# Encoder block: one half of W_out split early and kept in DRAM, and the other half's sixteen pieces spread over the attention heads

## The chip, the cores and the metric

The kernel runs on one core of a Trainium2 chip. The metric is the time of one execution in device microseconds (us); a lower one is better. The engines are called as in the profile: PE (TensorE), DVE (VectorE), ACT (ScalarE), POOL (GpSimd) and SP (SyncE, which here only issues transfers).

## What is computed

The reference is one block on x of 1024 rows and 1024 columns, in float32, cut here to what matters:

```python
x = LN1(alpha*x + 0.5 * (silu(x @ w_gate1) * (x @ w_up1)) @ w_down1)      # hidden width 4096
z = x @ w_in                                                              # q, k, v, two LRU inputs, forget gates
for h in range(8):                                                        # 8 heads of width 64
    s = q_h @ k_h.T / 8 + cum_h[t] - cum_h[s]                             # cum = cumsum(log_sigmoid(forget gate))
    fox[:, 64*h:64*h+64] = softmax(where(s <= t, s, -1e30)) @ v_h
lru = gelu(z_lg) * rg_lru(conv(z_lx))                                     # a linear recurrence, width 512
x = LN2(alpha*x + concat(fox, lru) @ w_out)                               # w_out: 1024 x 1024
x = LN3(alpha*x + 0.5 * (silu(x @ w_gate2) * (x @ w_up2)) @ w_down2)
```

`w_out` has two halves: its first 512 rows are multiplied with the attention's output (the attention half), its last 512 with that of the recurrence (the LRU half).

## The kernel before

**Products in three parts.** Each float32 operand is split into a high part (an ACT copy that casts to the fast type) and a low part (a DVE subtraction of the high part from the whole). `mm3` makes a product of three matmuls, high with high, high with low and low with high (L151 to L153). Splitting weights is thus work for ACT and DVE, and each split needs the weights' raw copy in SBUF first.

**Stages.** The program runs through FFN 1 (gate and up, then down), the mixer (input projections, the recurrence, the attention, the product with `w_out` and the second layer norm) and FFN 2. A framework lays each engine's instructions out in a fixed order by what each needs and when it was written; each engine then takes its own row in order and waits where an operand or a buffer isn't ready.

**Gate and up** (`gate_up`): sixteen pairs of 128-column blocks of the hidden width. Each pair is seven block products for gate and seven for up, each of 12 matmuls of 128x512. Their weights come as 1 MB loads into two raw buffers, are combined and split by ACT (L273) and DVE (L274) into a ring of 16 buffers (eight of high and low), and POOL stores the pair's results to DRAM (`h_d`, L543 and L544). While PE is busy with one pair, the weights of the next are made.

**Attention** (`attention`): 64 units, each a head h and a block i of 128 queries. Heads 0 to 5 run one after another, i from 7 down to 0; heads 6 and 7 are interleaved. A unit has these steps, and the names in brackets are used below.

- Scores (S h.i): matmuls L964 and L965 into PSUM; DVE adds the cumulated gates and takes the row's extreme (L970), ACT exponentiates (L971), POOL scales (L973). POOL also masks the diagonal block of the gates' row, which was loaded once per head (L968).
- Transposes (T h.i), three units later: up to 8 on PE (L984), copied and split by ACT (L988) and DVE (L989).
- Values (V h.i, for even i, two query blocks at once): matmuls L1000, then ACT (L1003) and DVE (L1004); for odd heads also a split of the finished pair of heads (L1007, L1008), which POOL stores to DRAM (`mix_d`, L1011).

Each head's q, k, v and gates are loaded by SP (L947 to L952) into one of two sets of buffers.

**The two halves of the output product.** The LRU half is 16 pieces (`fill`): 8 row blocks times 2 column halves, each of 4 times 3 = 12 matmuls of 128x512 (`down_tile`, L151 to L153) and one DVE addition. They depend on nothing in the attention and are written between the units: at units 0 to 4, then at every eighth unit plus 2, 3 and 4 (10 to 12, 18 to 20, 26 to 28) and at 34 and 35. The attention half is made at the end, in `out_tile`, as heads 6 and 7 get finished: again 16 pieces of 12 matmuls, M16 and on here; a row block's second piece is followed by its layer norm.

**W_out's attention half.** `out_w(w_out, 0)` loads its raw rows in two transfers of 1 MB (L929) and splits them in four steps at units 45, 47, 49 and 51, each a cast of 128x1024 by ACT (L143) and a subtraction by DVE (L144). The results lie in a pool of eight buffers, all of which hold the LRU half until that half's last pieces are through. At units 46, 48 and 52, SP loads the finished heads' parts back (`mix`, L1058), into another pool of eight that held the recurrence's output, the LRU half's other operand. SP takes its transfers in its own row as well: one that waits for a buffer holds up all behind it.

The functions before, with the line numbers of the profile:

Of the kernel before, what the change touches and what calls it, by code (L numbers as in the profile page):

```python
# [9 lines left out]
F32 = mybir.dt.float32  # L10
F32R = mybir.dt.float32r
# [6 lines left out]
P = 128  # L18
D = 1024
# [29 lines left out]
def f32(ap):  # L49
    return ap.bitcast(F32)  # L50


class Block:
# [202 lines left out]

        return raws, load

    def gate_up(self, wg, wu, h_d, rows, bank, tp, wsp, raws, later=None, aside=None):

# [256 lines left out]
        def halves(r):  # L519
            return r[:, 0:H], r[:, H:]  # L520

        pending = None
        for pair in range(FF // P // 2):
            if pair == 0:
                g0, h0, first, fifth, g1, h1, u = (self.row() for _ in range(7))
                homes = list(zip(halves(first), halves(first), halves(fifth)))
                gate, up = Matrix((g0, g1), *homes[0]), Matrix((h0, h1), *homes[1])
            else:
                g0, g1, uu, h0, h1, u = (self.row() for _ in range(6))
                gate, up = (Matrix(r, r[1][:, 0:H], x, r[0][:, H:]) for r, x in zip(((g0, g1), (h0, h1)), halves(uu)))  # L530
            def finish(pair=pair, g=(g0, g1), h=(h0, h1), u=u):
                for x, y in zip(h, g):
                    v.tensor_tensor(x, x, y, ALU.mult)
                (a11, a21), (a12, a22) = (halves(x) for x in h)
                s5 = g[0][:, 0:H]
                v.tensor_tensor(u[:, 0:H], a11, a22, ALU.add)
                v.tensor_tensor(u[:, H:], a21, a22, ALU.add)  # L537
                v.tensor_tensor(s5, a11, a12, ALU.add)
                v.tensor_tensor(a21, a21, a11, ALU.subtract)
                v.tensor_tensor(a12, a12, a22, ALU.subtract)  # L540
                d = h_d[pair // 4][:, pair % 4].rearrange("r p t -> p r t")
                for n, t in enumerate((*h, u)):
                    nc.gpsimd.dma_start(d[:, 2 * n:2 * n + 2], t.rearrange("p (r t) -> p r t", r=2))  # L543
                return nc.gpsimd.dma_start(d[:, 6], s5)  # L544

            def end(pair=pair, finish=finish):
                store = finish()
                if aside is not None and pair == 2:
                    with self.tc.issue_after(store.ins):
                        aside()  # L550

            if pair == 0:
                with self.tc.manual_schedule(engines=ENGINES) if later else nullcontext():
                    first_pair(gate, up)
                silu((g0, g1))
                end()
                continue
            for m, view in zip((gate, up), self.gu_views(wg, wu)):
                weights(pair, view, m.w)
            for m in (gate, up):  # L560
                m.one()
                if pending:
                    pending()
                for step in ("two", "six", "five", "seven", "three"):
                    getattr(m, step)()

                def pending(m=m, gate=gate, g=(g0, g1), end=end, last=pair == FF // P // 2 - 1):
                    m.four()
                    if m is gate:
                        silu(g)  # L570
                    elif not last:
                        end()
# [347 lines left out]

    def out_w(self, w_out, row0):

        wv = w_out.rearrange("(f p) d -> p f d", p=P)
        for c in range(2):
            r = self.raw([P, 2, D])
            f0 = row0 // P + 2 * c
            self.nc.sync.dma_start(r, wv[:, f0:f0 + 2, :])  # L929
            for j in range(2):  # L930
                yield tuple(t[:, 0, :] for t in self.split_ws(r[:, j:j + 1, :], 1))

    def attention(self, w_out, mixp, ln, normed):

        nc, v = self.nc, self.nc.vector
        mm = nc.tensor.matmul
        lru_tiles = list(zip(self.mix_lru, self.out_w(w_out, FOX)))
        with self.pool("att_p", 3) as pp, self.pool("att_t", 1) as tp, self.pool("att_pt", 6) as ptp, self.pool("att_qk", 2, side="right") as qkp:

            def load(h):  # L940
# [50 lines left out]
            def values(h, qt):  # L991
# [13 lines left out]
                if b:  # L1005
# [3 lines left out]
                    if qt == 0 and h < HEADS - 1:  # L1009
                        for l in range(2):  # L1010
# [4 lines left out]
            units = [(h, i) for h in range(HEADS - 2) for i in reversed(range(NT))]  # L1015
            units += [(6 + h, i) for h, i in ((0, 7), (0, 6), (0, 5), (0, 4), (1, 7), (1, 6), (0, 3), (0, 2),
                                              (1, 5), (1, 4), (0, 1), (0, 0), (1, 3), (1, 2), (1, 1), (1, 0))]
            tiles, mix, w_fox, w_steps = [], [], [], self.out_w(w_out, 0)
            MIXES = 46, 48, 52
            fill = [(i, d) for i in range(NT) for d in range(2)]  # L1020
            AHEAD = 3
# [9 lines left out]
            for n in range(len(units) + AHEAD + 1):  # L1031
                if n < len(units):
                    h, i = units[n]
                    if i == 5 and h < 6 or (h, i) == (6, 6):
                        heads[h + 1] = load(h + 1)
                    if i == NT - 1:
                        if h % 2 == 0:
                            outs[h // 2] = tp.tile([P, T], F32, tag="o", name=self.nm("o"))
                        else:
                            mixes[h // 2] = tuple(mixp.tile([P, T], F32R, tag="h", name=self.nm("mix")) for _ in range(2))  # L1040
                    ps[n] = probs(h, i)
                if 0 <= n - AHEAD < len(units):
                    to_pT(*units[n - AHEAD], ps.pop(n - AHEAD))
                if 0 <= n - AHEAD - 1 < len(units):
                    h, i = units[n - AHEAD - 1]
                    if i % 2 == 0:
                        values(h, i // 2)
                        if h == HEADS - 1:
                            tiles += [(i + 1, 0), (i + 1, 1), (i, 0), (i, 1)]
                if fill and (n < 2 or n % 8 in (2, 3, 4)):  # L1050
                    i, d = fill.pop(0)
                    self.down_tile(i, lru_tiles, 1.0, (d,))
                if 45 <= n < 53 and n % 2:
                    w_fox.append(next(w_steps))
                if n in MIXES:
                    mix.append(tuple(self.hp.tile([P, T], F32R, tag="h", name=self.nm("mix")) for _ in range(2)))
                    for l in range(2):
                        nc.sync.dma_start(f32(mix[-1][l]), mix_d[len(mix) - 1][l])  # L1058
                    if len(mix) == 3:
                        self.load_gb(*ln, [self.hp.tile([P, T], F32, tag="h", name=self.nm("gb")) for _ in range(2)])  # L1060
                if tiles:
                    out_tile()
# [4 lines left out]
def kernel(  # L1067
# [9 lines left out]
    xf = x[0]  # L1077
    h_d = [[blk.dram.tile([7, 4, P, H], F32, name=f"h{n}{q}_d") for q in range(4)] for n in range(2)]
    x2_d = blk.dram.tile([T, D], F32, name="x2_d")
    REST = ("s1", "s2", "s4", "s3")  # L1080

    with blk.pool("xl", side="right") as xl, blk.pool("x1") as x1, blk.pool("gu_t", 4) as tp, blk.pool("x22") as x22, \
            blk.pool("gu_ws", 16) as wsp, blk.banks() as bank, ExitStack() as inner:
        blk.open_blocks(x1, ("1",))
        blk.open_blocks(x22, ("22",))
        blk.open_blocks(xl, ("s3", "s1", "s2"))
        rows = [blk.row() for _ in range(4)]
        x2 = inner.enter_context(ExitStack())
        xp = x2.enter_context(blk.pool("x2", 4, side="right"))
        rows += [xp.tile([P, D], F32, tag="x2", name=blk.nm("x2")) for _ in range(4)]  # L1090

        def open_s4():
            x2.close()
            blk.open_blocks(inner.enter_context(blk.pool("s4", side="right")), ("s4",))

        raws, load = blk.first_raws(ffn1_w_gate[0], ffn1_w_up[0])
        warm = bank()
        for _ in range(12):
            nc.tensor.transpose(warm[:, 0:P], blk.ident, blk.ident)
        for i in range(NT):  # L1100
            if i == 4:
                load(0)
                load(1)
            nc.sync.dma_start(rows[i], xf[i * P:(i + 1) * P, :])

        finish = blk.gate_up(ffn1_w_gate[0], ffn1_w_up[0], h_d[0], rows, bank, tp, wsp, raws, open_s4, lambda: blk.mixer_consts(
            conv_w[0], conv_b[0], rg_wa[0], rg_ba[0], rg_wx[0], rg_bx[0], lru_lambda[0], b_forget[0], w_in[0]))
    with blk.psum():
        left = ExitStack()
        blk.wsp = left.enter_context(blk.pool("mx_ws", 8))  # L1110
        with blk.pool("dn_v", side="right") as vp, blk.pool("dn_w", side="right") as wp:
            first = []

            def hooks(norm):
# [3 lines left out]
                def columns(*offs):  # L1118
# [12 lines left out]
            blk.mixer_in(w_in[0], *first, [lambda i=i: blk.to_xT(i, False) for i in range(4, NT)])  # L1131
        mp = left.enter_context(blk.pool("mxp", 2))
        blk.fetched = None
        tiles, out_tile = blk.attention(w_out[0], mp, (ln2_g[0], ln2_b[0]),
                      lambda i: nc.gpsimd.dma_start(x2_d[(i + 4) % NT * P:((i + 4) % NT + 1) * P, :], blk.acc[i]))
        rows = blk.acc[4:] + blk.acc[:4]
        right = ExitStack()
# [59 lines left out]
```

## Time and profile before

| | before |
|---|---|
| median of 3 runs | 2354.17 us (2351.85 to 2358.68) |
| the profiled execution | 2350.71 us |
| its span in the trace | 2349.0 us, mean granted clock 0.998 |
| PE busy | 2305.3 us (98%) |
| DVE busy | 1631.3 us (69%) |
| ACT busy | 1011.6 us (43%) |
| POOL busy | 223.1 us (9%) |

The profiled execution has 1.7 us outside its span. The clock column of the views, PEclk, is the share of full speed that TensorE was granted. "Idle before" with an engine, a tile and a line says how long an engine stood still ahead of an instruction, and which other instruction it had waited for. A view by windows cuts the span at given times and gives each engine's busy time in each stretch, then the granted clock, the DMA engines' busy share and their rate.

### The profile page before, as it was taken

Reading aid. Unit: us, or ns where it says so; the run is one execution under the profiler, and the core shown is the slowest. Engines: PE = TensorE matmul, PEld = TensorE weight load, DVE = VectorE, ACT = ScalarE, POOL = GpSimd, SP = SyncE. Lnnn points to the kernel's source line nnn. Section 1 sums busy time; section 2 is a strip of 40 time slices with the busy share of each in tenths; the row PEclk is TensorE's granted clock in tenths of the full one; section 3 lists DMA queues with packets and bytes.
Section 4 is the critical chain, followed back from the end, with each engine's and each line's share of the span. In section 5 each row is a group of like instructions: output and inputs, shape, how many; then the busy total and the mean of one; then the engine's idle time right before and its main releaser. Section 6 shows DMA issues by size and latency. Waiting matters only on the chain.

```text
span 2349.0 us, 28311 instructions
## 1 busy us (share of the span) xinstructions
PE 2305.3 (98%) x10721; PEld 1914.4 (81%) x10721; DVE 1631.3 (69%) x2512; ACT 1011.6 (43%) x1587; POOL 223.1 (9%) x364
## 2 busy tenths in 40 slices
PE   9999999999999999999999899999999999999997
PEld 7788888888888888888878677888888888788886
DVE  7766566666567888766657899665656566478787
ACT  5443333434344345544446745434333333344341
POOL 0020000000000000111134510000000000000000
PEclk9999999999999999999999999999999999999999
DMA  3433232323466434232365812332323232564532
GB/s 121 139 90 126 91 117 85 117 86 117 145 240 215 161 115 120 60 109 91 118 174 149 237 54 86 103 117 86 118 92 126 86 117 86 198 247 156 196 108 90
DMA packets 175832, 298.93 MB, mean 127 GB/s; under 512 B 8192, under 2 KB 100672, under 8 KB 175696
## 3 DMA queue, kind: packets, MB, share of 16 engines
q1 hardware_dynamic: 152624, 218.15, 29.2%
q0 software_dynamic: 23072, 78.97, 9.1%
q8 instruction: 84, 1.38, 0.2%
q14 instruction: 52, 0.43, 0.1%
HBM read 214.22 MB, written 82.87 MB: 126 GB/s over the span
## 4 chain that ended last, share of the span: by engine, by line
PE 91%; DVE 5%; issue 1%; DMA 1%; ACT 1%; POOL 1%; SPq 0%; POOLq 0%; ACTq 0%; DVEq 0%
PE x L153 10%; PE x L152 9%; PE x L151 9%; PE b L152 7%; PE b L153 7%; PE b L151 7%; PE s L153 6%; PE s L152 6%; PE s L151 6%; PE a L151 6%; PE a L153 6%; PE a L152 5%; PE a L1000 1%; PE a L984 1%; PE a L873 1%
## 5 line engine op out<-in xcount | busy, mean ns | idle before, releaser
L273 ACT CAST ws<-t 128x512 fp32r<-128x512 f32 x240 | 148.9, 623 | 389.5 <-PE b L152 269.1
L273 ACT CAST ws<-raw 128x512 fp32r<-128x512 f32 x180 | 111.8, 623 | 260.0 <-PE x L152 256.6
L274 DVE TENSOR_TENSOR ws<-raw,ws 128x512 fp32r<-128x512 f32 x180 | 123.8, 688 | 142.7 <-ACT ws L273 139.3
L274 DVE TENSOR_TENSOR ws<-t,ws 128x512 fp32r<-128x512 f32 x240 | 164.4, 686 | 70.5 <-ACT ws L273 68.5
L151 PE MATMUL b<-As,ws 128*128 128x512 f32 x512 | 199.8, 390 | 3.0 <-ACT As L309 2.8
L151 PE MATMUL a<-ws,ws 128*128 128x512 f32 x512 | 199.2, 390 | 2.1 <-ACT ws L607 1.6
L151 PE MATMUL x<-As,ws 128*128 128x512 f32 x512 | 199.5, 390 | 1.0 <-ACT ws L273 1.0
L153 PE MATMUL x<-As,ws 128*128 128x512 f32 x512 | 199.4, 390 | 0.7 <-DVE ws L274 0.6
L152 PE MATMUL a<-ws,ws 128*128 128x512 f32 x512 | 199.5, 390 | 0.5 <-DVE ws L608 0.5
L152 PE MATMUL b<-As,ws 128*128 128x512 f32 x512 | 199.4, 390 | 0.2 <-DVE As L315 0.2
L153 PE MATMUL b<-As,ws 128*128 128x512 f32 x512 | 199.4, 389 | 0.0
L152 PE MATMUL x<-As,ws 128*128 128x512 f32 x512 | 199.2, 389 | 0.0
L153 PE MATMUL a<-ws,ws 128*128 128x512 f32 x512 | 199.2, 389 | 0.0
L151 PE MATMUL x<-A,ws 128*128 128x512 f32 x496 | 193.2, 390 | 1.1 <-ACT ws L273 1.1
L153 PE MATMUL x<-A,ws 128*128 128x512 f32 x496 | 193.3, 390 | 0.9 <-DVE ws L315 0.7
L152 PE MATMUL x<-A,ws 128*128 128x512 f32 x496 | 193.0, 389 | 0.0
L607 ACT CAST ws<-raw 128x1024 fp32r<-128x1024 f32 x112 | 117.4, 1050 | 161.5 <-PE a L152 87.8
L543 POOL DMA_DIRECT2D h_d<-row x96 | 68.8, 719 | 1155.6 <-DVE row L537 1116.5
L608 DVE TENSOR_TENSOR ws<-raw,ws 128x1024 fp32r<-128x1024 f32 x112 | 136.4, 1220 | 54.0 <-ACT ws L607 53.4
L151 PE MATMUL s<-ws,ws 128*128 128x512 f32 x384 | 149.5, 389 | 0.0
L153 PE MATMUL s<-ws,ws 128*128 128x512 f32 x384 | 149.4, 389 | 0.0
L152 PE MATMUL s<-ws,ws 128*128 128x512 f32 x384 | 149.4, 389 | 0.0
(248 smaller groups left out, 5227.8 us busy)
## 6 DMA issues: line engine op xcount, KB each, us to landing
raw<-h_d SPq DMA_DIRECT2D x56, 1024.0 KB, 5.5
h_d<-row POOLq DMA_DIRECT2D x96, 512.0 KB, 3.7
wd<-in_ffn_w_down_dram SPq DMA_DIRECT2D x32, 1024.0 KB, 7.8
raw<-in_ffn_w_gate_dram SPq DMA_DIRECT2D x30, 1024.0 KB, 5.5
raw<-in_ffn_w_up_dram SPq DMA_DIRECT2D x30, 1024.0 KB, 5.4
h_d<-row POOLq DMA_DIRECT2D x32, 256.0 KB, 2.6
raw<-in_w_in_dram SPq DMA_DIRECT2D x16, 512.0 KB, 5.2
row<-in_x_dram SPq DMA_DIRECT2D x12, 512.0 KB, 8.9
```

The lines of the kernel that those rows point to most:

```text
L151: mm(out, ah, bh, start=first, stop=False, skip_group_check=goes_on)
L152: mm(out, ah, bl, start=False, stop=False, skip_group_check=goes_on)
L153: mm(out, al, bh, start=False, stop=last, skip_group_check=goes_on)
L273: nc.scalar.copy(hi, src)
L274: v.tensor_tensor(lo, src, f32(hi), ALU.subtract)
L543: nc.gpsimd.dma_start(d[:, 2 * n:2 * n + 2], t.rearrange("p (r t) -> p r t", r=2))
L607: nc.scalar.copy(hi, src)
L608: self.mark = v.tensor_tensor(lo, src, f32(hi), ALU.subtract)
L873: nc.tensor.matmul(pa[:, 0:width], xl, wh[:, 0:width], start=False, stop=k == KT - 1)
L984: nc.tensor.transpose(pa[:, (j % 4) * P:(j % 4 + 1) * P], p[:, j * P:(j + 1) * P], self.ident)
L1000: mm(pv[:, ps], vt[:, j, :], pts[h, qt][j // 4][l][:, j % 4, ps], start=j == 0 and l == 0, stop=j == last and l == 1)
```

## The change

The first FFN's `gate_up` gets the attention half of `w_out` as a `spare`. At pairs 5 and 9, behind the pair's weights, `split_spare` loads 1 MB of it into a raw buffer, splits it in four blocks of 128x512 with the same ACT and DVE instructions as the weights, into buffers of the same ring, and POOL stores the eight results (256 KB each) to a new DRAM tensor, `fox_d`. Together that is 2 loads, 8 casts, 8 subtractions and 16 stores. At units 45, 47, 49 and 51, `out_w_parts` now loads finished parts from `fox_d`, 512 KB for the high and 512 KB for the low, in place of the raw loads, casts and subtractions. And the LRU half's 16 pieces are written at units 0 to 5 and then at every fourth, 8, 12, and so on to 44.

```diff
+        def split_spare(c):
+            w, w_d = spare
+            r = self.raw([P, KT, 2 * P]).rearrange("p k c -> p (k c)")
+            nc.sync.dma_start(r.rearrange("p (f d) -> p f d", f=2), w.rearrange("(f p) d -> p f d", p=P)[:, 2 * c:2 * c + 2])
+            for j in range(2):
+                for d in range(2):
+                    cols = slice(j * D + d * H, j * D + (d + 1) * H)
+                    for l, t in enumerate(parts(r[:, cols].rearrange("p (k c) -> p k c", k=4))):
+                        nc.gpsimd.dma_start(w_d[2 * c + j, l][:, d * H:(d + 1) * H], f32(t).rearrange("p k c -> p (k c)"))
...
                 weights(pair, view, m.w)
+            if spare and pair in (5, 9):
+                split_spare(pair // 8)
...
+    def out_w_parts(self, w_d):
+        w = [self.wsp.tile([P, 4 * VW], F32R, tag="ws", name=self.nm("w"))[:, 0:D] for _ in range(2)]
+        for l in range(2):
+            self.nc.sync.dma_start(f32(w[l]), w_d[l])
+        return w
...
-            tiles, mix, w_fox, w_steps = [], [], [], self.out_w(w_out, 0)
+            tiles, mix, w_fox = [], [], []
...
-                if fill and (n < 2 or n % 8 in (2, 3, 4)):
+                if fill and (n < 6 or n % 4 == 0):
                     i, d = fill.pop(0)
                     self.down_tile(i, lru_tiles, 1.0, (d,))
                 if 45 <= n < 53 and n % 2:
-                    w_fox.append(next(w_steps))
+                    w_fox.append(self.out_w_parts(fox_d[len(w_fox)]))
```

Lines move down: L273 becomes L274, the attention's L964 becomes L984, L984 becomes L1004, L1000 becomes L1020 and L1058 becomes L1078.

How this moves the rows of instructions is shown at three places, first before, then after. On PE at the turn from head 4 to head 5, `s` are scores, `a<-ident,p` transposes, `a<-pt,v` values and `a<-w,mix` the first of the 12 matmuls of a piece. Before, nothing stands between the transposes of T5.6 and T5.5 and the values V5.6:

```order
L964 MATMUL s_10935<-kh_10555,q_10554 128x384
L965 MATMUL s_10935<-kl_10556,q_10554 128x384
L984 MATMUL a_10929<-ident,p_10813 128x128 x3
L984 MATMUL a_10951<-ident,p_10858 128x128 x4
L984 MATMUL a_10958<-ident,p_10858 128x128 x2
L1000 MATMUL a_10963<-pt_10885,v_10557 128x256
```

After:

```order
L984 MATMUL s_10988<-kh_10594,q_10593 128x384
L1004 MATMUL a_10968<-ident,p_10852 128x128 x3
L985 MATMUL s_10988<-kl_10595,q_10593 128x384
L151 MATMUL a_10974<-w_9312,mix_7298 128x512
...
L1004 MATMUL a_11004<-ident,p_10897 128x128 x4
L1004 MATMUL a_11011<-ident,p_10897 128x128 x2
L1020 MATMUL a_11016<-pt_10924,v_10596 128x256
```

The sixteenth and last piece (M15) now stands there; before, it stood one head earlier, and the rows from there to M16 hold no piece in either. Counted over the rows, the stretches from one V h.6 to the next hold 3, 3, 3, 2 and 0 pieces before (from V0.6 to V5.6), and 3, 2, 2, 2 and 2 after.

On SP, around the loads of head 7 (`q`, `kh`, `kl`, `v`, `cum`; the last is the gates' row), before:

```order
L950 DMA v_10844<-v_d 128x8x128
L255 DMA raw_12046<-in_ffn_w_gate_dram 128x4x256
...
L947 DMA q_11085<-q_d 64x1024
...
L950 DMA v_11088<-v_d 128x8x128
L952 DMA cum_11084<-cum_d 128x1024
L255 DMA raw_12047<-in_ffn_w_up_dram 128x4x256
L1058 DMA mix_11231<-mix_d 128x1024
L1058 DMA mix_11232<-mix_d 128x1024
L90 DMA gb_11235<-in_ln_g_dram 128x1024
```

After:

```order
L970 DMA v_10883<-v_d 128x8x128
L950 DMA w_11037<-fox_d 128x1024
L950 DMA w_11038<-fox_d 128x1024
L1078 DMA mix_11064<-mix_d 128x1024
...
L1078 DMA mix_11132<-mix_d 128x1024
L967 DMA q_11136<-q_d 64x1024
...
L972 DMA cum_11135<-cum_d 128x1024
L950 DMA w_11182<-fox_d 128x1024
...
L950 DMA w_11248<-fox_d 128x1024
L1078 DMA mix_11280<-mix_d 128x1024
```

Before, the four transfers of mix parts 0 and 1 stand ahead of head 6's loads, and the raw loads of the next FFN between the heads. After, four transfers of `w` and four of `mix` (eight of 512 KB) stand directly ahead of head 7's loads, and four of `w` and two of `mix` behind them; the next FFN's loads stand earlier in the row.

On PE at V6.6, where the scores S7.7 and S7.6 are head 7's first, before:

```order
L1000 MATMUL a_11187<-pt_11111,v_10557 128x256
...
L984 MATMUL a_11218<-ident,p_11102 128x128 x3
L964 MATMUL s_11204<-kh_11086,q_11085 128x512
...
L965 MATMUL s_11240<-kl_11087,q_11085 128x384
L984 MATMUL a_11258<-ident,p_11142 128x128 x4
L984 MATMUL a_11265<-ident,p_11142 128x128 x2
L1000 MATMUL a_11270<-pt_11169,v_10844 128x256
...
L964 MATMUL s_11289<-kh_10842,q_10841 128x512
```

After:

```order
L1020 MATMUL a_11236<-pt_11162,v_10596 128x256
...
L1004 MATMUL a_11267<-ident,p_11153 128x128 x4
L1004 MATMUL a_11307<-ident,p_11191 128x128 x4
L1020 MATMUL a_11319<-pt_11218,v_10883 128x256
...
L1004 MATMUL a_11350<-ident,p_11209 128x128 x4
L984 MATMUL s_11253<-kh_11137,q_11136 128x512
...
L985 MATMUL s_11289<-kl_11138,q_11136 128x384
L984 MATMUL s_11338<-kh_10881,q_10880 128x512
```

Head 7's eight score matmuls have moved from ahead of V6.6 to behind V6.6 and the transposes T6.4; from S6.3 on both rows agree.

More of the change, by code (lines that the diff above doesn't have):

```diff
@@ L257, in first_raws, with gate_up @@
         return raws, load
-    def gate_up(self, wg, wu, h_d, rows, bank, tp, wsp, raws, later=None, aside=None):
+    def gate_up(self, wg, wu, h_d, rows, bank, tp, wsp, raws, later=None, aside=None, spare=None):
         nc, v = self.nc, self.nc.vector
@@ L919, in mixer_in, with out_w, attention @@
                     self.forget()
-    def out_w(self, w_out, row0):
-        wv = w_out.rearrange("(f p) d -> p f d", p=P)
+    def out_w(self, w_out):
+        wv = w_out[FOX:, :].rearrange("(f p) d -> p f d", p=P)
         for c in range(2):
             r = self.raw([P, 2, D])
-            f0 = row0 // P + 2 * c
-            self.nc.sync.dma_start(r, wv[:, f0:f0 + 2, :])
+            self.nc.sync.dma_start(r, wv[:, 2 * c:2 * c + 2, :])
             for j in range(2):
                 yield tuple(t[:, 0, :] for t in self.split_ws(r[:, j:j + 1, :], 1))
-    def attention(self, w_out, mixp, ln, normed):
+    def out_w_parts(self, w_d):
[3 more added lines that the diff above has]
+        return w
+    def attention(self, w_out, fox_d, mixp, ln, normed):
         nc, v = self.nc, self.nc.vector
         mm = nc.tensor.matmul
-        lru_tiles = list(zip(self.mix_lru, self.out_w(w_out, FOX)))
+        lru_tiles = list(zip(self.mix_lru, self.out_w(w_out)))
         with self.pool("att_p", 3) as pp, self.pool("att_t", 1) as tp, self.pool("att_pt", 6) as ptp, self.pool("att_qk", 2, side="right") as qkp:
@@ L1079 @@
     x2_d = blk.dram.tile([T, D], F32, name="x2_d")
+    fox_d = blk.dram.tile([FOX // P, 2, P, D], F32, name="fox_d")
     REST = ("s1", "s2", "s4", "s3")
@@ L1106 @@
         finish = blk.gate_up(ffn1_w_gate[0], ffn1_w_up[0], h_d[0], rows, bank, tp, wsp, raws, open_s4, lambda: blk.mixer_consts(
-            conv_w[0], conv_b[0], rg_wa[0], rg_ba[0], rg_wx[0], rg_bx[0], lru_lambda[0], b_forget[0], w_in[0]))
+            conv_w[0], conv_b[0], rg_wa[0], rg_ba[0], rg_wx[0], rg_bx[0], lru_lambda[0], b_forget[0], w_in[0]),
+            (w_out[0][0:FOX, :], fox_d))
     with blk.psum():
@@ L1133 @@
         blk.fetched = None
-        tiles, out_tile = blk.attention(w_out[0], mp, (ln2_g[0], ln2_b[0]),
+        tiles, out_tile = blk.attention(w_out[0], fox_d, mp, (ln2_g[0], ln2_b[0]),
                       lambda i: nc.gpsimd.dma_start(x2_d[(i + 4) % NT * P:((i + 4) % NT + 1) * P, :], blk.acc[i]))
```

## The prediction

> **What bounds the kernel now.** I read the page first, for who is busy.
>
> ```profile
> span 2349.0 us, 28311 instructions
> PE 2305.3 (98%) x10721; PEld 1914.4 (81%) x10721; DVE 1631.3 (69%) x2512; ACT 1011.6 (43%) x1587; POOL 223.1 (9%) x364
> ```
>
> PE is the bound: of 2349.0 us it stands still for 43.7. The change leaves PE's 10721 matmuls as they are, so it can only gain where PE stands still, and lose where PE doesn't yet. The next view cuts windows: first 50 us in the middle of the first FFN's gate and up (columns: PE, PEld, DVE, ACT, POOL busy, granted clock, share of the DMA engines, GB/s).
>
> ```profile
> 350.00:400.00 50.00, 50.00 (x222) 41.44 (x221) 29.62 (x44) 20.12 (x33) 2.72 (x4) 1.00 0.24 80
> ```
>
> PE never rests there, and ACT, DVE, POOL and the DMA engines are free for half of the time or more. Then the attention, cut where each head's V h.6 begins: V1.6 to V2.6 is the first row, V4.6 to V5.6 the fourth; the last two go from V5.6 over V6.6 to M16, the first piece of the attention half.
>
> ```profile
> 1230.29:1252.53 22.24, 21.94 (x140) 19.39 (x138) 17.78 (x47) 14.60 (x36) 9.73 (x18) 1.00 0.62 166
> 1252.53:1274.51 21.98, 21.80 (x140) 19.31 (x138) 16.26 (x43) 13.41 (x32) 8.29 (x16) 1.00 0.51 121
> 1274.51:1295.40 20.89, 20.07 (x129) 17.42 (x127) 17.64 (x46) 16.56 (x38) 8.98 (x17) 1.00 0.66 178
> 1295.40:1312.90 17.50, 14.57 (x99) 12.23 (x99) 16.35 (x42) 14.32 (x34) 9.70 (x13) 1.00 0.98 260
> 1312.90:1330.73 17.83, 15.85 (x104) 13.40 (x105) 15.00 (x44) 14.00 (x36) 9.23 (x17) 1.00 0.87 232
> 1330.73:1345.41 14.68, 11.87 (x84) 9.96 (x83) 10.48 (x26) 9.79 (x21) 6.87 (x12) 1.00 0.74 269
> ```
>
> The rows with three pieces of the LRU half are full: PE idles 0.30 and 0.18 us. The row with two idles 0.82, the one with none 2.93 (17.50 - 14.57), and the last two 1.98 and 2.81. So 9.0 us of PE's rest lie in the six rows. The waits on PE in the fourth to sixth row and the end of the third say what for:
>
> ```profile
> PE s L964 <- DVE m L970: 4.5, 9, 1.5
> PE a L984 <- POOL p L973: 1.6, 3, 0.5
> ```
>
> Scores wait for DVE to have read the scores before them (a PSUM buffer), transposes for POOL's scaling. Softmax limits a head without pieces, PE one with three.
>
> **Part 1: the splits in gate and up.** Rows of the page for the same instructions and the stores:
>
> ```profile
> L273 ACT CAST ws<-raw 128x512 fp32r<-128x512 f32 x180 | 111.8, 623 | 260.0 <-PE x L152 256.6
> L274 DVE TENSOR_TENSOR ws<-raw,ws 128x512 fp32r<-128x512 f32 x180 | 123.8, 688 | 142.7 <-ACT ws L273 139.3
> L543 POOL DMA_DIRECT2D h_d<-row x96 | 68.8, 719 | 1155.6 <-DVE row L537 1116.5
> raw<-in_ffn_w_gate_dram SPq DMA_DIRECT2D x30, 1024.0 KB, 5.5
> h_d<-row POOLq DMA_DIRECT2D x32, 256.0 KB, 2.6
> ```
>
> Added are 8 casts of 0.623 us (5.0), 8 subtractions of 0.688 (5.5), 16 issues of 0.719 on POOL (11.5), two loads (5.5 to land) and 16 stores (2.6). Per pair it is half of that. A product is 12 matmuls, 50.00/222 x 12 = 2.70 us, a pair 14 of them, 37.8 us. In it DVE is free for 41% (20.38/50.00), 15.4 us against 2.75 added, and ACT for 60%, 22.6 against 2.5. The cover is the ring: eight pairs of high and low, so weights stand up to seven products, 18.9 us, ahead of PE. The spare takes four of the eight until their stores have landed, some 2.6 us after the last issue; three products, 8.1 us, remain as cover. The raw buffer that it borrows delays a weight load by about one landing, 5.5 us, also less than 8.1. POOL's eight stores stand between the results of two pairs, whose rows are needed next a pair later. I take 0. If the cover fails at one of the two pairs, that pair's four casts show, 2.5 us: the bounds are 0 and +2.5, and none below, since PE has nothing to give back there.
>
> **Part 2: pieces spread over heads 1 to 5.** A piece alone, cut as a window, and the splits that leave:
>
> ```profile
> 1262.08:1264.83 2.75, 2.75 (x14) 2.26 (x14) 1.98 (x7) 2.31 (x5) 2.65 (x5) 1.00 1.01 206
> L143 ACT CAST w<-raw x4: 1032/1041/1052, 1291.5 to 1301.1; 128x1024 fp32r<-128x1024 f32 x4
> L144 DVE TENSOR_TENSOR w<-raw,w x4: 1204/1206/1209, 1292.9 to 1307.4; 128x1024 fp32r<-128x1024 f32 x4
> ```
>
> The window runs from the piece's first matmul to just behind its last, 2.75 us (its 14 records include two neighbours); by part 1's spacing the 12 take 2.70, and I use 2.73. The four heads take 22.24 + 21.98 + 20.89 + 17.50 = 82.61 us with 3, 3, 2 and 0 pieces and the four splits (4 x 1.04 on ACT, 4 x 1.21 on DVE). Afterwards each has two pieces and no split. If PE stays full, one costs 21.98 - 2.73 = 19.25, four 77.0: -5.6. If each costs what the two-piece row costs now, 4 x 20.89 = 83.6: +1.0. That row holds casts and a subtraction of the splits, which go, so I stay nearer to 19.25 and add 0.55 for the softmax waits that two pieces don't cover, a third of the way: 19.80 x 4 = 79.2, **-3.4**.
>
> **Part 3: from V5.6 to M16.** Here no piece and no split is moved; what changes is SP's row. Timeline rows of PE, SP, POOL and DVE:
>
> ```profile
> 1326.81 0.37 SPq L950 DMA_DIRECT2D v<-v_d  x1
> 1327.28 0.53 SPq L952 DMA_DIRECT2D cum<-cum_d  x1
> 1332.47 0.29 POOL L968 TENSOR_SCALAR_AFFINE_SELECT cum<-cum 128x128 f32<-128x128 f32 x1 [0.59 <-DMA cum<-cum_d]
> 1333.63 1.21 DVE L970 CUSTOM_DVE_ANT_0 p<-s,cum 128x1024 f32<-128x1024 f32 x1
> 1334.77 0.68 DVE L989 TENSOR_TENSOR pt<-a,pt 128x512 fp32r<-128x512 f32 x1
> 1334.90 0.50 PE L964 MATMUL s<-kh,q 128*128 128x512 f32 x1 [1.48 <-DVE m L970]
> 1336.51 0.44 PE L964 MATMUL s<-kh,q 128*128 128x384 f32 x1 [0.88 <-DVE m L970]
> 1345.41 0.45 PE L151 MATMUL a<-w,mix 128*128 128x512 f32 x1
> ```
>
> Head 7's gates' row is landed at 1332.4, 19.5 us after V5.6; its mask and R7.7 (the DVE step at 1333.63) follow, and S6.3 waits 1.48 for that. This is where a late transfer shows. After, the last LRU piece M15 stands just before V5.6 and frees the buffers that SP's eight transfers wait for; they start about 1.4 us ahead of V5.6 (half a piece). Queued until the gates' row: w and mix, 8 x 524 KB = 4.19 MB; q, kh and kl, 1.57 MB; v and the gates' row, 1.05 MB: 6.81 MB. Rates, by window:
>
> ```profile
> 1292.00:1296.00 4.00, 3.48 (x25) 2.87 (x24) 4.00 (x9) 3.61 (x7) 1.48 (x4) 1.00 1.06 388
> 1300.00:1304.00 4.00, 3.74 (x25) 3.15 (x24) 4.00 (x12) 3.50 (x9) 1.95 (x3) 1.00 0.98 253
> 1304.00:1308.00 4.00, 3.50 (x25) 3.02 (x25) 4.00 (x11) 3.61 (x9) 2.50 (x5) 1.00 1.03 218
> ```
>
> The first is the mix transfers of before, the others a head's loads with the DMA engines full. So 4.19/388 = 10.8 us, 1.57/218 = 7.2, 1.05/253 = 4.1: 22.1, less 1.4, and 1.2 for issue and completion (an estimate: v and the gates' row, issued from 1326.81, took 5.6 us to 1332.4, 1.5 more than their 4.1; part of that runs beside the queue): 21.9 after V5.6, 2.4 later than now. The subtractions of T6.4 now stand ahead of R7.7, which takes 0.68 out behind it: **+1.7**. S7.7 and S7.6 leave their place ahead of V6.6 and run in that wait. Bounds: with loads no later than now and DVE free, the waits of 1.48 and 0.88 go, -2.4; at 260 GB/s for all (the head row with the DMA engines at 0.98) 26.2 - 0.2 = 26.0, 6.5 later, less 0.7: +5.8. Behind the gates' row are still w 2 and 3 and mix 2, 3.15 MB, in all 9.96; at the mean of the sum, 6.81/22.1 = 308 GB/s, they land 32.1 after V5.6, before the third matmul group of M16 (32.5 + 1.4 + 1.7 = 35.6): hidden.
>
> [...]
>
> **Sum.** 0 - 3.4 + 1.7 = -1.7 us: 2349.0 for the profiled execution (2350.71). That one lies below the three runs; the median of all four (2351.85, 2354.17, 2358.68, 2350.71) is 2353.0, and the forecast stands on it: **2351.3**. About 0.3%, 7 us, is what a measurement of this kernel can tell from no change.
>
> **The rivals.**
>
> *Full packing.* Four heads at 19.25 and no late transfer: -5.6 - 2.4 = -8.0, 2345.0. For it: PE was full with three pieces at the same softmax, and ACT and DVE lose 4.2 and 4.8 us of splits just there. Against it: a two-piece row that idles 0.82, and waits in single halves of a head that a piece elsewhere doesn't fill. It decides if the heads come under about 19.5 and the row lands in time. 0.24.
>
> *The transfer queue behind the last piece.* SP's row starts half a piece before V5.6, not a head earlier, and at the 218 GB/s of a full stretch the gates' row lands 6.81/218 - 0.2 = 31.0 after V5.6, 11.5 late; the last of 9.96 MB lands at 45.5 where M16 wants it at 33.9, 11.6 late. With part 2 that is +8.2, 2361.2. It costs from 346 GB/s down (19.7 us for the 6.81 MB) and is over 7 us slower from 225 down. For it: two windows of head loads at 253 and 218, and nothing else in the queue to hide behind. Against it: 388 for large rows, which are two thirds of this queue. [...] 0.13.
>
> *Nothing is gained.* The two-piece heads cost 20.89 as now (+1.0) and the row is in time or as late as forecast (-0.7 to +1.7): +0.3 to +2.7, some 2354.5. For it: PE's rest in heads 4 and 5 may be a chain of S, DVE, ACT, POOL and T that a piece merely shifts. That the change doesn't do what it says is excluded by the rows: the pieces and splits did move. 0.11.
>
> **The numbers.** Forecast 0.52. Forecast and "nothing" both stay within 7 us: same 0.63; packing makes faster 0.24, the queue slower 0.13. The range goes down to full packing, 2345.0, and up to 2359: 2353.0 with part 3 at its upper bound of +5.8 and nothing from part 2. It leaves out the queue's 2361.2 and what little lies below packing.
>
> **What would show it.** In gate and up: PE 50.00 of 50 around pairs 5 and 9, no wait for ws over 1 us. Heads 2 to 5 between 19.2 and 20.5 us, PE idle under 1 us each, and PE's waits for the DVE step (L970, now L990) down to half. V5.6 to M16: 34.2 us against 32.5, the gates' row of head 7 landing about 21.9 after V5.6. Wrong would be: PE waits in gate and up; heads at 20.9; the row landing after 26 or before 19; or M16's matmuls waiting for w or mix.

## The result, and the profile after

| | before | after |
|---|---|---|
| median of 10 runs each | 2354.16 us (2350.67 to 2358.68) | 2360.28 us (2358.18 to 2365.5) |
| ratio, with its 95% interval | | 1.0031 (1.0024 to 1.0039) |
| the profiled execution | 2350.71 us | 2363.75 us |

The change costs 6 to 7 us. The forecast was 2351.3 us, 1.7 less than the 2353.0 that it took for before; the measured time lies 1.3 us above the end of the range (2359). The traced execution of before is about as fast as the fastest of the ten, and that of after is the second slowest of its ten, so the two traces differ by 13 us and not by the 6 or 7 of the medians.

The page of after, span and busy times: PE's matmuls are the same 10721.

```profile
span 2362.0 us, 28411 instructions
PE 2311.9 (98%) x10721; PEld 1919.5 (81%) x10721; DVE 1632.3 (69%) x2516; ACT 1011.4 (43%) x1591; POOL 228.4 (10%) x380
```

I laid the two traces over each other matmul by matmul. Two places account for nearly all. The first is in gate and up, at pair 9. PE's timeline there:

```profile
399.10 0.39 PE L153 MATMUL b<-As,ws 128*128 128x512 f32 x1
...
401.82 0.39 PE L153 MATMUL x<-As,ws 128*128 128x512 f32 x1
405.59 0.79 PE L151 MATMUL b<-As,ws 128*128 128x512 f32 x1 [3.39 <-ACT row L505]
406.19 0.63 PE L152 MATMUL b<-As,ws 128*128 128x512 f32 x1
```

PE waits 3.39 us, and the matmuls behind take 0.63 in place of 0.39. The waiting product is `three`. It adds to the PSUM bank `m.z`, which `five` has filled (its last matmul is the one at 399.10) and which a copy on ACT (L505) has to read first; between them stands one product, `seven`. From the kernel:

```python
            def five(m):
                m.z = m.product("t1", "s1")
                nc.scalar.copy(m.s5, m.z)                 # L505
            ...
            def three(m):
                v.tensor_tensor(m.c[1], m.product("22", "s4", m.z), m.u, ALU.add)
```

So PE waits for that copy: it starts 0.05 us after the copy's end. The copy is late because of what stands ahead of it in ACT's row. ACT's timeline, then DVE's subtraction that goes with its first cast, POOL's last stores and SP's weight loads:

```profile
382.98 0.62 ACT L274 CAST ws<-raw 128x512 fp32r<-128x512 f32 x1 [1.61 <-PE x L152]
...
397.87 0.62 ACT L274 CAST ws<-raw 128x512 fp32r<-128x512 f32 x1 [2.83 <-DMA fox_d<-ws]
...
403.92 1.14 ACT L274 CAST ws<-t 128x512 fp32r<-128x512 f32 x2 [4.42 <-DMA fox_d<-ws]
404.96 0.58 ACT L505 COPY row<-b 128x512 f32<-128x512 f32 x1
```

```profile
383.87 0.68 DVE L275 TENSOR_TENSOR ws<-raw,ws 128x512 fp32r<-128x512 f32 x1
```

```profile
395.49 1.61 POOL L532 DMA_DIRECT2D fox_d<-ws  x3 [1.36 <-DVE ws L275]
```

```profile
384.58 0.37 SPq L289 DMA_DIRECT2D raw<-in_ffn_w_gate_dram  x1
395.40 0.37 SPq L289 DMA_DIRECT2D raw<-in_ffn_w_up_dram  x1
```

The view of transfers from 385 to 410 us gives them with their median time to land:

```profile
fox_d<-ws POOLq DMA_DIRECT2D x8, 256.0 KB, 3.4
raw<-in_ffn_w_up_dram SPq DMA_DIRECT2D x1, 1024.0 KB, 9.5
raw<-in_ffn_w_gate_dram SPq DMA_DIRECT2D x1, 1024.0 KB, 5.4
```

ACT's casts for the next pair's weights wait for ring buffers whose stores haven't landed. The last three stores are issued at 395.49 and behind, just as the 1 MB load of up starts; they take 5.6, 7.8 and 8.1 us to land (the first three 2.3 to 2.5), and the load takes 9.5 in place of 5.4. The second of the three lands at 403.8; at 403.92 ACT's row goes on with two casts, and behind them the copy runs. The weights of the waiting product itself had long been there: `three` takes the last weights but one of pair 9, which are the cast at 382.98 and the subtraction at 383.87, some 22 us before PE uses them. The load of up is late as well: before, it stands at 383.48, and the spare's raw buffer has taken its place.

The second place is the end of the attention. The windows of after, from V1.6 by heads to V5.6, then V6.6 and M16 (columns as before; the third from the end is the granted clock):

```profile
1239.35:1260.82 21.47, 19.97 (x130) 17.32 (x128) 17.15 (x47) 14.38 (x36) 9.69 (x18) 1.00 0.58 145
1260.82:1280.22 19.40, 19.14 (x125) 16.84 (x124) 15.24 (x43) 13.25 (x32) 8.26 (x16) 1.00 0.66 166
1280.22:1301.70 21.48, 19.98 (x129) 17.32 (x128) 17.16 (x47) 14.38 (x36) 9.64 (x18) 1.00 0.55 146
1301.70:1321.09 19.39, 19.13 (x125) 16.86 (x124) 15.25 (x43) 13.26 (x32) 8.25 (x16) 1.00 0.72 188
1321.09:1337.90 16.81, 13.88 (x99) 12.00 (x97) 14.48 (x41) 13.94 (x35) 7.22 (x13) 1.00 1.02 307
1337.90:1359.89 21.99, 16.67 (x90) 13.47 (x91) 12.09 (x30) 10.06 (x22) 6.80 (x14) 0.77 0.86 296
```

The first four rows, from V1.6 to V5.6, take 81.74 us against 82.61. V5.6 to M16 takes 38.80 against 32.51, with a granted clock of 0.77 in its second row. POOL's mask of head 7's gates' row and what waits behind it:

```profile
1346.85 0.29 POOL L988 TENSOR_SCALAR_AFFINE_SELECT cum<-cum 128x128 f32<-128x128 f32 x1 [7.80 <-DMA cum<-cum_d]
```

```profile
1341.90 0.70 PE L984 MATMUL s<-kh,q 128*128 128x512 f32 x2 [1.31 <-DMA kh<-k_d]
...
1348.46 0.80 PE L984 MATMUL s<-kh,q 128*128 128x512 f32 x1 [3.14 <-DVE m L990]
```

The row is there 25.8 us after V5.6 (19.6 before), and S6.3 waits 3.14 us (1.48 before).

### The profile page after: what moved, and what is told of

Same layout as the page of the kernel before. It is cut to its first block, busy times and chain, and to the rows that moved or that the text cites. A ratio compares the mean times of both kernels' runs of the same rounds, so it can differ in the third digit from the quotient of the medians.

```text
span 2362.0 us, 28411 instructions
## 1 busy us (share of the span) xinstructions
PE 2311.9 (98%) x10721; PEld 1919.5 (81%) x10721; DVE 1632.3 (69%) x2516; ACT 1011.4 (43%) x1591; POOL 228.4 (10%) x380
## 4 chain that ended last, share of the span: by engine, by line
PE 87%; DVE 6%; issue 4%; ACT 2%; DMA 1%; POOL 1%; SPq 0%; POOLq 0%; DVEq 0%; ACTq 0%
PE x L153 9%; PE x L151 9%; PE x L152 9%; PE b L152 7%; PE b L151 7%; PE b L153 7%; PE s L153 6%; PE s L152 6%; PE s L151 6%; PE a L151 6%; PE a L153 6%; PE a L152 5%; PE a L1020 1%; PE a L1004 1%; DVE row L198 1%
## 5 line engine op out<-in xcount | busy, mean ns | idle before, releaser
L274 ACT CAST ws<-t 128x512 fp32r<-128x512 f32 x240 | 148.7, 623 | 389.8 <-PE b L152 264.9
L274 ACT CAST ws<-raw 128x512 fp32r<-128x512 f32 x188 | 116.7, 623 | 261.4 <-PE x L152 254.3
L275 DVE TENSOR_TENSOR ws<-raw,ws 128x512 fp32r<-128x512 f32 x188 | 129.1, 688 | 142.0 <-ACT ws L274 138.3
```

Source lines behind the costliest of these rows:

```text
L274: nc.scalar.copy(hi, src)
L275: v.tensor_tensor(lo, src, f32(hi), ALU.subtract)
```

## The experiments

Theory A names two costs: stores that hold the ring at pair 9, and a late transfer queue ahead of M16. Its rivals are named in the expectations. All ratios are to the kernel before on the same chip, with 95% intervals.

**after_again**: the changed kernel, unaltered.

> The changed kernel, unaltered, for a second trace. Theory A (two costs: stores that hold the ring of gate and up at pair 9, and a late transfer queue ahead of M16): about 1.003 of before, and again a wait of PE for ACT near 401 us of some 3 us with a half granted clock behind it (+5 to +7 us by 420 us), and V5.6 to M16 again some 38 us against 32.5. Rival B (the wait at pair 9 belongs to that one execution; the tail alone makes the loss): the same time, but no wait over 1 us in gate and up. Rival C (the clock alone: half-clock windows fall by chance): the waits are there in both traces but with different clock losses.

2360.35 us, 1.0022 (1.0014 to 1.0031). The wait at pair 9 is there again (2.8 us), V5.6 to M16 takes 36.9 and the gates' row comes 23.9 us after V5.6. So rival B falls: both waits belong to the program and not to one execution. What rival C gave is there too, on top of the waits: the half clock behind pair 9 lasts 6.83 us in the first trace (0.50 from 404.78 to 411.61) and 3.41 in this one (0.50 from 405.08 to 408.49).

**pieces_only**: before, with the new places of the pieces.

```diff
-                if fill and (n < 2 or n % 8 in (2, 3, 4)):
+                if fill and (n < 6 or n % 4 == 0):
```

> Only the new places of the LRU half's pieces; W_out's attention half is loaded raw and split at units 45 to 51 as before. Theory A: no stores in gate and up, so nothing there; heads 1 to 5 about 82 to 83 us (82.6 before), with the splits now waiting for M15 a head later: 0 to +4 us in the stretch to M16, in all 0 to +4 us, 1.000 to 1.002. Rival B (the late last piece makes the loss): +5 to +8 us, 1.002 to 1.0035. Rival D (the spreading is worth its 3 us and only the rest costs): -2 to -4 us.

1.0005 (0.9997 to 1.0014). V1.6 to V5.6 takes 81.73, the same as after: the splits wait for M15, and most of them slide behind V5.6, out of these rows (casts from 1313.4 to 1321.9, V5.6 at 1314.99). A wait of 4.2 us shows up in the pieces behind M16 instead:

```profile
PE a L151 <- ACT mix L1007: 4.2, 1, 4.2
```

Neither rival B nor D: spreading alone gains nothing and costs little.

**split_only**: after, with the old places of the pieces.

```diff
-                if fill and (n < 6 or n % 4 == 0):
+                if fill and (n < 2 or n % 8 in (2, 3, 4)):
```

> Only the split in gate and up and the loads of parts; the pieces stand as before, so that the last is through a head earlier. Theory A: the wait at pair 9 stays (+4 to +7), the tail is free of ACT's and DVE's splits and its queue starts a head earlier, 0 to -4: in all 0 to +7, 1.000 to 1.003. Rival B (the tail's late queue is all): -2 to -4 us, 0.998 to 0.999.

1.0001 (0.9993 to 1.001), at the low end of what A allowed. The wait at pair 9 is there (3.56 us). The windows from V3.6 to V5.6, with two pieces and with none:

```profile
1280.34:1300.58 20.24, 19.84 (x130) 17.42 (x128) 16.62 (x45) 14.40 (x35) 8.99 (x17) 1.00 0.64 175
1300.58:1316.80 16.22, 14.78 (x101) 12.59 (x101) 13.72 (x42) 13.62 (x35) 7.97 (x15) 1.00 1.03 302
```

These were 20.89 and 17.50 with the splits: the splits' leaving is worth 0.65 and 1.28 us, in all four rows 1.9 (80.67 against 82.61). With the pieces spread, the four rows take 81.74 for the same eight pieces, 1.1 more. And V5.6 to M16 takes 33.8, not 38.8.

**split_unused**: the split and its stores in gate and up, the attention of before.

> The split in gate and up with its loads and stores, whose results nobody reads; the attention is that of before. What it costs above before is the price of part 1 alone. Theory A: +4 to +7 us, 1.002 to 1.003, with a wait of PE over 2 us at pair 9. Rival B: within 1 us of before.

1.0024 (1.0015 to 1.0033), with a wait of 3.1 us at pair 9. Rival B falls: part 1 costs some 6 us by itself (by the interval 3.5 to 8).

**unused_no_stores**: as split_unused, but without the 16 stores.

```diff
-                    for l, t in enumerate(parts(...)):
-                        nc.gpsimd.dma_start(w_d[2 * c + j, l][:, d * H:(d + 1) * H], ...)
+                    parts(...)
```

> Gate and up load and split W_out's attention half, but nothing is stored (the 16 stores to DRAM are left out; the results are not used, the attention is that of before). Theory A, in its sharper form after the first four runs: at pair 9 the ring's buffers are held by stores that land late because a weight load runs beside them, so without stores PE doesn't wait at pair 9, and the kernel is within 2 us of before (0.9995 to 1.0008). Rival E (it is not the stores: the weight load of up that is issued late, since the spare holds a raw buffer, is what PE waits for): the wait of about 3 us at pair 9 stays, 1.001 to 1.0025.

0.9997 (0.9988 to 1.0006). The waits list has no entry left from 100 to 620 us. The window from 400 to 412 us, first split_unused, then this kernel:

```profile
400.00:412.00 12.00, 8.95 (x40) 7.10 (x39) 8.32 (x13) 3.87 (x7) 0.00 (x0) 1.00 0.35 120
```

```profile
400.00:412.00 12.00, 12.00 (x55) 9.93 (x54) 7.74 (x12) 4.26 (x8) 0.00 (x0) 1.00 0.30 93
```

With loads, casts, subtractions and the raw buffer still in it, PE is full: 12.00 of 12.00 us against 8.95. The spare still takes the raw buffer that up's load would have. So it is the stores, and rival E (the late weight load) falls as a cause by itself.

**spread_splits**: the split in eight steps at pairs 4 to 11, one block each, loaded into a buffer for differences instead of a raw buffer.

```diff
+            f, d = divmod(c, 2)
+            r = tp.tile([P, 4, P], F32, tag="t", name=self.nm("t"))
+            nc.sync.dma_start(r, w[f * P:(f + 1) * P, cols].rearrange("p (k c) -> p k c", k=4))
+            for l, t in enumerate(parts(r)):
+                nc.gpsimd.dma_start(w_d[f, l][:, cols], f32(t).rearrange("p k c -> p (k c)"))
...
-            if spare and pair in (5, 9):
-                split_spare(pair // 8)
+            if spare and 4 <= pair < 12:
+                split_spare(pair - 4)
```

> The changed kernel, with the split in eight steps of one 128x512 block at pairs 4 to 11, each loaded by itself (256 KB) into one of the buffers for differences, so that no raw buffer is taken and only one pair of the ring waits for stores at a time. Theory A: no wait of PE over 1 us in gate and up, 3 to 6 us faster than the changed kernel: 0.9995 to 1.001. What stays is the tail: V5.6 to M16 still near 38 us. Rival B (the tail is all): 1.002 to 1.003 as now.

1.0006 (0.9997 to 1.0014). The stores' time to land and the window of gate and up:

```profile
DMA to landing us min/median/max: 2.3/2.4/2.5
```

```profile
400.00:412.00 12.00, 12.00 (x54) 9.93 (x54) 6.89 (x10) 3.46 (x6) 0.00 (x0) 1.00 0.29 87
```

No wait is left in gate and up, while V5.6 to M16 stays at 38.3. As A said. This step takes away both the load beside the stores and the row of eight stores, so it doesn't tell which of the two counts for how much.

**head7_first**: after, with w and mix loaded later, so that four transfers instead of eight stand ahead of head 7's loads.

```diff
-            MIXES = 46, 48, 52
+            MIXES = 51, 52, 53
...
-                if 45 <= n < 53 and n % 2:
+                if 50 <= n < 54:
```

> The changed kernel with the loads of w and mix written at units 50 to 53, so that four of them instead of eight stand ahead of head 7's loads. Theory A: head 7's gates' row lands 4 to 6 us sooner after V5.6 (20 to 22 in place of 25.7), S6.3 waits under 1.5 us, V5.6 to M16 33 to 35 us in place of 38; gate and up as in the changed kernel: 1.000 to 1.0015. Rival F (the order doesn't matter, M16 waits for the same bytes in any order): M16 is reached as late as now, with the wait moved to w or mix, 1.002 to 1.003.

1.0009 (0.9999 to 1.0018). POOL's mask, and the windows from V5.6 and from V6.6 to M16:

```profile
1339.83 0.29 POOL L988 TENSOR_SCALAR_AFFINE_SELECT cum<-cum 128x128 f32<-128x128 f32 x1 [0.65 <-DMA cum<-cum_d]
```

```profile
1321.23:1338.04 16.81, 15.45 (x108) 13.44 (x106) 14.49 (x41) 13.66 (x34) 7.20 (x13) 1.00 0.85 234
1338.04:1353.79 15.75, 13.24 (x85) 11.36 (x83) 11.97 (x30) 10.54 (x22) 6.78 (x14) 0.89 1.02 397
```

The row is there 18.6 us after V5.6 and the stretch takes 32.56, as before the change. The bytes are the same; only what M16's chain needs first now comes first. Rival F falls.

**early_end**: after, with the last LRU piece eight units earlier.

```diff
-                if fill and (n < 6 or n % 4 == 0):
+                if fill and (n < 8 or n % 4 == 0):
```

> The changed kernel with the pieces at units 0 to 7 and then every fourth up to 36, so that the last LRU piece is through eight units (one head) earlier. Theory A: the queue of w and mix starts a head earlier and is split by head 6's loads; V5.6 to M16 falls to 31 to 34 us, and with heads 4 and 5 on two pieces and one piece fewer the stretch V1.6 to V5.6 is 80 to 82 us: in all 1.000 to 1.0015, the cost of pair 9 left. Rival F: 1.002 to 1.003, since the DMA engines are full in this stretch whatever comes first.

1.0024 (1.0014 to 1.0034): not in A's range, and in rival F's. V0.6 to V1.6 and V4.6 to V5.6 of this kernel:

```profile
1216.72:1244.35 27.63, 27.36 (x163) 23.72 (x162) 17.48 (x45) 13.18 (x32) 8.26 (x16) 1.00 0.40 96
```

```profile
1306.73:1322.95 16.22, 14.78 (x103) 12.54 (x101) 13.65 (x41) 13.56 (x33) 7.28 (x14) 1.00 1.03 290
```

Two more pieces in the first stretch cost 5.2 us (27.63 against 22.40), and two fewer in the last return 3.2 (19.39 against 16.22). And the queue is only split, not shorter: w 1 and mix 1 still stand ahead of head 7's loads, and head 6's v and gates' row are issued just ahead of those (1318.99 and 1319.46). Head 7's gates' row comes 21.3 us after V5.6, S6.3 waits 2.5 us, and V5.6 to M16 takes 36.4. With four transfers ahead, as in head7_first, that is 2.7 us later than there; no run isolates why. F's reason, that the order doesn't matter while the DMA engines are full, doesn't fit head7_first.

**spread_old**: spread_splits with the old places of the pieces.

> W_out's split in eight steps in gate and up, and the pieces at their old units: the only parts of the change that have not cost in the runs so far. Theory A: the split at the old pieces was 1.0001 of before with the wait at pair 9 still in it; without that wait 5 to 6 us faster: 0.9973 to 0.9985, no wait over 1 us in gate and up, V1.6 to V5.6 about 80.7 us. Rival B (the wait in gate and up never mattered to the median, only the tail): 1.0000 as before.

2351.33 us, 0.999 (0.9982 to 0.9999): the direction that A gave, less than its size (0.9973 to 0.9985). Rival B's 1.0000 lies just outside the interval.

**spread_head7**: spread_splits and the later loads of head7_first.

> The new places of the pieces, with both costs taken away: the split in eight steps, and four in place of eight transfers ahead of head 7's loads. Theory A: the two savings add: the changed kernel's 1.0025 to 1.003 less 0.002 (stores) less 0.0015 to 0.002 (tail): 0.9985 to 0.9998; V1.6 to V5.6 81.7 us, V5.6 to M16 33 us. Rival G (the pieces' places cost by themselves): 1.0005 or more.

1.0000 (0.9991 to 1.0009). No wait in gate and up, V5.6 to M16 32.5. With both costs gone the change is worth nothing. The median lies between what A gave (up to 0.9998) and what G gave (from 1.0005), and the interval reaches into both, so this run doesn't decide between them.

**spread_head7_old**: the same with the old places of the pieces.

> As spread_old, with the later loads of w and mix too. Theory A: the old pieces end a head earlier, so the queue was no longer late; the order is worth 0 to 3 us beside spread_old: 0.9965 to 0.9985. Rival F: no better than spread_old or worse, since mix and w then come late at M16: 0.998 to 1.000.

2349.63 us against 2353.35 on the same chip, 0.998 (0.9971 to 0.9989): faster than before, and with it than the change. The value lies in A's range and at the end of F's, so it doesn't part them, and its interval overlaps that of spread_old. The windows from V4.6 to V5.6, V6.6 and M16:

```profile
1297.98:1314.18 16.20, 14.78 (x100) 12.56 (x100) 13.72 (x42) 13.62 (x35) 7.92 (x15) 1.00 1.03 293
1314.18:1331.59 17.41, 15.23 (x102) 13.25 (x103) 15.33 (x43) 13.33 (x34) 9.10 (x17) 1.00 0.93 251
1331.59:1346.39 14.80, 13.33 (x85) 11.52 (x84) 11.18 (x28) 10.45 (x22) 6.01 (x13) 0.88 0.98 353
```

## Why the prediction was wrong, point by point

The terms as forecast and as measured in the traces:

| term | forecast (bounds) | after | after_again | without its cause |
|---|---|---|---|---|
| part 1, gate and up (the 200 matmuls around pair 9: 45.33 us before) | 0 (0 to +2.5) | +6.5 | +5.0 | 0.0 (spread_splits) |
| part 2, V1.6 to V5.6 (82.61) | -3.4 (-5.6 to +1.0) | -0.9 | -0.9 | -1.9 (split_only) |
| part 3, V5.6 to M16 (32.51) | +1.7 (-2.4 to +5.8) | +6.3 | +4.4 | 0.0 (head7_first) |

**Part 1 failed, and made the loss.** The step was "the spare takes four of the eight until their stores have landed, some 2.6 us after the last issue; three products, 8.1 us, remain as cover". Two things in it were wrong.

The 2.6 was the landing time of stores in the kernel before. The change itself sets a 1 MB load beside the last stores: it takes a raw buffer, so up's load is issued when the spare's raw is free, which is just when the spare's last results are stored. The last three stores then take up to 8.1 us. I had counted the raw buffer's delay and the stores apart, and not together.

And the cover was counted in weights, which did not run out. What ran out was the time for a copy in ACT's row. The casts that wait for the stores stand there ahead of the copy L505 of `five`. Its product is through at 399.5 and the next product but one needs the bank at about 402, so the cover was one product, 2.7 us, and not three. In after, PE starts 0.05 us after the end of this copy (405.54 and 405.59), and in all six traces with the wait it is the copy that PE waits for.

At pair 5 the same meeting did no harm, by little:

```profile
243.09 0.37 SPq L289 DMA_DIRECT2D raw<-in_ffn_w_up_dram  x1
```

```profile
247.82 1.14 ACT L274 CAST ws<-t 128x512 fp32r<-128x512 f32 x2 [2.04 <-DMA fox_d<-ws]
248.87 0.58 ACT L505 COPY row<-b 128x512 f32<-128x512 f32 x1
```

The last two stores take 5.2 and 7.4 us there and up's load 8.0, but the store that held the casts had been issued half a us ahead of the load (at 242.54). The copy ends at 249.45, PE starts `three` at 249.72, and the matmuls around pair 5 take as long as before.

Experiments with and without the stores (1.0024 and 0.9997) put the price at some 6 us; in the six traces the term is 3.4 to 6.5, of which 1.9 to 3.6 are PE's wait. The bound of +2.5 came from counting the casts of one pair; the wait is set by the stores' landing and by ACT's row, and in after and after_again a half clock came on top (0.50 for 6.83 and 3.41 us), in split_only and split_unused none (1.00 up to 410 and 412 us).

**Part 2 was overrated.** The step was that a head with two pieces and no splits takes 19.80, whichever head it is. The four rows, with the number of pieces in brackets; split_only and after differ in the pieces' places alone:

| from | before | split_only | after |
|---|---|---|---|
| V1.6 | 22.24 (3) | 22.23 (3) | 21.47 (2) |
| V2.6 | 21.98 (3) | 21.98 (3) | 19.40 (2) |
| V3.6 | 20.89 (2) | 20.24 (2) | 21.48 (2) |
| V4.6 | 17.50 (0) | 16.22 (0) | 19.39 (2) |

The second and fourth rows came out as forecast, near the floor of 19.25. There taking the third piece out saves 2.58 us, nearly the whole 2.73. The first and third rows didn't: PE idles 1.50 us in each, taking the third piece out saves 0.76, and in the third row the same number of pieces at new places costs 1.24 more. These are the rows that also hold the split of a finished pair of heads (DVE and ACT have four instructions more each), and in each of them scores wait 0.9 us for DVE's read; that the split is the cause is not shown. Over both:

```profile
PE s L984 <- DVE m L990: 1.8, 2, 0.9
```

The two pieces that went into the empty row cost 3.17 there. The 17.50 from which I read an idle PE held two casts and three subtractions of the splits; without them the row takes 16.22. In all, what gains is that the splits leave (-1.9); the spreading gives 1.1 of it back.

**Part 3 had the right mechanism and too small a size**, in the one trace beyond its bound of +5.8. I put the gates' row at 21.9 us after V5.6; it came at 25.8 and 23.9. The window from SP's first w to the row, in after:

```profile
1318.44:1346.85 28.41, 22.26 (x141) 18.45 (x139) 19.48 (x54) 16.86 (x43) 10.11 (x19) 0.94 1.03 306
```

The rate is what I had summed (306 against 308 GB/s), but 28.41 us of it are 8.7 MB, not 6.81: 0.7 MB are POOL's store of the third part of mix, and some 1.1 MB belong to transfers that were issued ahead of the first w or behind the row. The term counted the bytes of one stretch of one queue; the DMA engines, full at 1.03, moved others in the same time. The step that was off is "4.19/388 = 10.8 us" for w and mix: the last of the eight is landed 17.3 us after the first issue. The six loads of q and k take 7.2 us more, as forecast, and v and the row 3.8 (4.1). The queue also starts 2.6 us ahead of V5.6 and not 1.4. S6.3's wait grows by 1.7 us, S7.7 waits 1.31 for kh, and behind it the granted clock is 0.50 for 10.24 us (from 1343.45).

**The rivals.** "The transfer queue behind the last piece" (0.13) came nearest: the late row decided part 3, at 4.4 to 6.3 us where it had 11.6, joined by part 1, which no rival held. PE waited for no transfer of w or mix. "Nothing is gained" was near on the heads: 20.4 us on average, where it had 20.89. The -0.7 that it gave part 3 with the row in time no run shows: with the row 18.6 and 18.7 us after V5.6, the stretch took 32.56 (head7_first) and 32.21 (spread_head7_old), where it had taken 32.51. "Full packing" held in two rows of four, and the row landed late.

**What stays open.** The terms of the traces add up to 11.9 us (after) and 8.5 (after_again), the medians to 5 to 7. The traced execution of before lost nothing to a half clock until the last 10.4 us of its span (0.50 from 2338.58) and is some 3.5 us under its median; that of after has 3.41 us at 0.50 from 8.83 and again from 1193.26, outside the three parts. How often each wait costs a half clock over many executions wasn't measured. In split_unused the term of part 1 is 3.4 us in the trace, where the median lies 6 above before. Nor does a run isolate why spread_old gained 2 us and not the 5 that split_only and the stores' price gave.

## What to carry to other kernels

Work moved under a full engine is free only as long as the buffers that it borrows come back in time: price a borrowed ring slot by the landing of its store beside the loads that run then (here up to 8.1 us in place of 2.3 to 2.5). Then look at what stands behind the waiting instruction in its engine's row; the shortest cover counts, and here it was that of a copy and not that of the weights. When transfers wait for one event, put first in the queue what the chain behind it needs first; in the traces here the order alone was worth the whole loss of the last stretch (32.56 us in head7_first, 38.80 in after, 32.51 before). Before spreading work to fill gaps, price a piece in each kind of stage by itself: here taking one out saved 2.6 us in one kind of row and 0.8 in the other, two put into the empty row cost 3.2, and new places alone cost 1.2.

## What the runs showed of the hardware

Up to 2350 us, the trace of after has four stretches with a granted clock of 0.50: 3.41 us from 8.83, 6.83 from 404.78, 3.41 from 1193.26 and 10.24 from 1343.45. Their starts lie 116, 231 and 44 times 3.413 us apart. The wait at pair 9 and what follows, cut at the second of them:

```profile
401.37:404.78 3.41, 0.84 (x4) 0.37 (x2) 0.47 (x1) 0.86 (x2) 0.00 (x0) 1.00 0.37 148
404.78:411.61 6.83, 6.02 (x14) 4.76 (x15) 4.88 (x8) 1.90 (x4) 0.00 (x0) 0.50 0.11 22
```

In split_only, a slightly longer wait (3.56 us) at the same place, cut at the same width of 3.41 us:

```profile
399.76:403.17 3.41, 1.49 (x7) 0.91 (x5) 0.69 (x1) 0.04 (x1) 0.00 (x0) 1.00 0.58 230
403.17:406.59 3.42, 1.78 (x8) 1.48 (x9) 2.25 (x4) 2.11 (x4) 0.00 (x0) 1.00 0.01 4
```

In after the wait fell mostly into one window (PE busy 0.84 of 3.41), and the next 6.83 us ran at 0.50; in split_only it was spread over two (1.49 and 1.78), and the clock stayed at 1.00. Nearly the same wait cost 6.5 us in the one and 3.9 in the other. With the trace of after cut in the same way from 5.42 to 2350 us, the two stretches of 3.41 us at full clock with the least PE work (1.41 us from 5.42, 0.84 from 401.37) were both followed by 0.50. Of the next four, with 1.61 to 1.76, two were (1.61 from 1189.85, 1.73 from 1340.03) and two were not (1.72 from 1333.21, 1.76 from 25.90); of those with more, none was. So in these traces the busy share alone doesn't tell what follows.
